# Output products by pairs, cache rows by way of GpSimd and DRAM copies, and a fixed order for the first up units

## The chip, the cores and the metric

The kernel runs on one core of a Trainium2 chip. Its time is the device time of one execution in microseconds (us), the median of several runs. The engines of a core are TensorE (PE), VectorE (DVE), ScalarE (ACT), GpSimd (POOL) and SyncE (SP). SP computes nothing; it issues DMAs, as POOL and ACT also can. Each engine works through its own instructions in a fixed order and waits at the first one whose inputs are not there.

## What is computed

The reference is one layer of a streaming encoder over 1024 prompt frames and 64 sample frames (1088 tokens, width 1024), in float32:

```python
xn = rmsnorm(x, g_mix)
cb, cc, ch, q, k, v, ga, gb = split(xn @ w_in)          # widths 6 x 512, 2 x 1024
ya = (cb * causal_conv(cc * ch, prefix)) @ w_conv_out
o  = band_attention(q, k_all, v_all, rel_bias)          # 8 heads of 64, own chunk and 8 before
yb = o @ w_attn_out
x  = x + (sigmoid(ga) * ya + sigmoid(gb) * yb) @ w_out
h  = rmsnorm(x, g_ffn)
x  = x + (silu(h @ w_ff1) * (h @ w_ff3)) @ w_ff2
y  = rmsnorm(x, g_final)
```

For the sample frames, keys and values are 512 cached rows followed by the 64 new ones. The newest 512 rows of each are outputs too (`cache_k_sample`, `cache_v_sample`): 448 old rows and 64 new ones.

## The kernel before, in words

Every operand is held as two float32r halves, a rounded one and a rest, and every product is three matmuls (rounded by rounded, and the two mixed ones). `split` (L120) makes the halves: a cast on ACT (L122), then a subtraction on DVE (L123).

The big products use a Strassen scheme with seven products in place of eight. `STEPS` (L128) orders them 1, 2, 6, 7, 5, 4, 3; each is 24 matmuls of 272 columns in `run` (L240). `Unit` loads 256 columns of a weight matrix into one of two `raw` buffers (L180), and `Unit.prep` (L192) makes the sums and splits of each step's weights. Banks of PSUM carry the keys A, B and D; a bank that is added to again must first have been copied out (`shot`, L226). The steps 6, 7 and 5 use the sums `xs` or `tt` of the tokens' four quarters.

Phase 1 (L485 to L759) normalises nine token tiles, computes v, and then runs twelve units: q, k, cc, ch, gb and cb. The SBUF block `scr` is cut by hand into places: SNAP, STAGE (four slots for rows on their way to DRAM), CC and UT (two slots each); `slot` (L331) hands a list's places out in turn. In the units of q and k, `cache_load` (L681) brings 128 old cache rows into a UT slot by way of SP. `cache_tile` (L686) stores them to the cache outputs (L691, POOL) and writes split v rows (`put_v`, L344, through a CC slot) and transposed, split k rows (L700, through the next CC slot) to DRAM. Beside units 4 and 5, `bias_tables` (L113) loads a table for two heads (L117) into a STAGE slot and stores it to DRAM (L118), both on SP. Fourteen `warm` matmuls run before the first tile (L504); `pvv` is the product for v (L475), for which `whv` holds weights.

Phase 2 (L762 to L1020) computes gates (`gate`, L771: four pieces of 272 columns, each evacuated by ACT at L779 into one of two `st` buffers and stored by POOL at L780) and interleaves the attention (L949). Before the last three gate blocks it loads the conv branch u (L1005), the attention rows o (L1008) and the softmax factors rc (L1012, two buffers), and makes the operand `ob` of their product (L1015, L1016). `gates_in` (L975) loads the gates back.

Phase 3 (L1025 to L1044) merges: for each of eight blocks m of 128 channels, four pieces ya (12 matmuls each, 48 in all) from the conv branch, then four pieces yb from `ob`. DVE multiplies them with the gates, adds, and the sum is split into `mg` (and `ms` for the sample tokens). `plan` (L313) lists the weights in the order of use; `next_w` prepares one product ahead of the block in use.

Phase 4 multiplies with w_out (L1084), adds the residual, normalises (`second`, L1129; L1143) and transposes the tiles again (`turned`, L1146; `xt`, L1153). `second_half` (L1172) makes the sums of quarters; for the tiles at columns 256 and 384 most of them are put off (`rest`). The memory pool `wp` holds what this needs; afterwards `hp` reuses its memory.

Phase 5 is the up stage: 22 units, alternately of w_ff1 (a0, a1, ...) and w_ff3 (b0, b1, ...), the first two started while the last two token tiles are still on their way (L1399 to L1422). Products of the two (`hidden_done`, L1234) are combined, split into `hq` (three buffers) and stored to `h_d` by POOL (L1245). Phase 6 is the down stage (L1526), whose weights lie in `ring` parts (L1284), four of 1024 columns in each ring; part 3 is first filled for pair 3, in the second half of the first block.

The order of each engine's instructions is not the order of the text. A planner orders them when the kernel is built: each instruction becomes ready, by the planner's own estimates of durations, when its inputs and buffers are there, and each engine takes the ready one that stands first in the text. `tc.issue_after(x)` holds the instructions of its block behind x on x's own engine. Buffers of a pool can be taken when each earlier tile on the same memory has been released.

Of the kernel before, what the change touches and what calls it, by code (L numbers as in the profile page):

```python
# [15 lines left out]
P = 128  # L16
# [22 lines left out]
WARM = 14  # L39
# [26 lines left out]
def encoder_kernel(ctx: ExitStack, tc: tile.TileContext, ins, outs):  # L66
# [46 lines left out]
    def bias_tables(j, t):  # L113

        t = t.rearrange("p (h n) -> p h n", h=2)
        src = ins["bias_ext"][2 * j, 384:]
        nc.sync.dma_start(t, bass.AP(tensor=src.tensor, offset=src.offset, ap=[[0, P], [768, 2], [1, 384]]))  # L117
        nc.sync.dma_start(bias_d[2 * j : 2 * j + 2].rearrange("h (p n) -> p h n", n=384), t)  # L118

    def split(hi, lo, src):  # L120

        a = act.copy(hi, src)  # L122
        vec.tensor_tensor(lo, src, hi.bitcast(F32), op=ALU.subtract)  # L123
        return a.ins
# [13 lines left out]
    def both(t, c, n, src):  # L138
        split(t[:, 0, :, c : c + n], t[:, 1, :, c : c + n], src)
# [36 lines left out]
    class Unit:  # L176
# [9 lines left out]
        def plain(self, p, src):  # L186
            self.w[p] = [
                ws.tile([P, 4, P], F32R, tag=t, name=f"{t}{self.nm}_{p}") for t in ("wh", "wl")
            ]
            split(*self.w[p], src)  # L190
# [28 lines left out]

    def run(unit, x, banks, snaps, done, ahead):  # L220


        nm = unit.nm
        ps, snap = {}, {}

        def shot(key, src):  # L226
            s = snaps(key, f"s{nm}_{key}").rearrange("p (j n) -> p j n", j=2)
            act.copy(s, src)
            snap[key] = s

        for si, p in enumerate(STEPS):
            key = {1: "A", 6: "A", 5: "A", 3: "A", 2: "B", 7: "D", 4: "D"}[p]
            if key not in ps:
                ps[key] = banks("A" if key == "A" else "BD", f"{key}{nm}")
            t = ps[key]
            hi, lo = unit.w[p]
            for k in range(4):
                for n, (w, l) in enumerate(((hi, 0), (hi, 1), (lo, 0))):
                    for j in range(2):
                        mm(  # L240
                            t[:, j, :HN], w[:, k, :], x[p][:, l, k, j * HN : (j + 1) * HN],
                            start=p in (1, 2, 7) and k == 0 and n == 0,
                            stop=k == 3 and n == 2, skip_group_check=p in (6, 5, 4, 3),
                        )
# [83 lines left out]
    SNAP, STAGE, CC, UT = [544 * i for i in range(5)], [2720, 3808, 9312, 10400], [4896, 5988], [7080, 8172]  # L328
    turn = {}
# [74 lines left out]


# [94 lines left out]
    warm = bank1("A", "warm")  # L500
    ones = mspool.tile([P, 2, 512], F32R, tag="ms", name="ones")[:, 0]
    act.copy(ones, cols[:, 13:14].to_broadcast([P, 512]))
    for n in range(WARM):
        mm(warm[:, n % 2], ones[:, :P], ones, start=True, stop=True)  # L504
# [3 lines left out]
    split_wv(0, mixed[0])  # L508
    split_wv(1, mixed[0])
# [171 lines left out]
    def cache_load(i):  # L681
        cts[i] = ct = slot(UT, 2 * ATT)
        nc.sync.dma_start(ct[:, :ATT], ck[i * P : (i + 1) * P])
        nc.sync.dma_start(ct[:, ATT:], cvv[i * P : (i + 1) * P])

    def cache_tile(i):  # L686
        ct = cts[i]
        a = 0 if i else TS
        row = i * P + a - TS
        for nm, o in (("k", 0), ("v", ATT)):  # L690
            nc.gpsimd.dma_start(outs[f"cache_{nm}_sample"][row : row + P - a], ct[a:, o : o + ATT])  # L691
# [72 lines left out]
    st_pool = pg_stack.enter_context(tc.tile_pool(name="st_pool", bufs=2, reuse_waits="tile"))  # L764
# [210 lines left out]
    def gates_in(m):  # L975
        sg = {}
        for o, n in PIECES:
            for nm, src in (("ga", ga_d), ("gb", gb_d)):
                t = sg[nm, o] = mp.tile([P, HN], F32, tag=nm, name=f"{nm}{m}_{o}")
                nc.sync.dma_start(t, src[m * P : (m + 1) * P, o : o + n])  # L980
        return sg
# [11 lines left out]
    for i in range(4, len(GATES)):  # L993
        gate_w[i] = next_w()
        if i == len(GATES) - LAST:
# [7 lines left out]
            sg = gates_in(0)  # L1003
            for k in range(4):
                nc.sync.dma_start(u.t[:, :, k].bitcast(F32), u_d[k])  # L1005
            for k in range(4):
                o = ob.t[:, 0, k].bitcast(F32)
                nc.sync.dma_start(o, o_d[k * P : (k + 1) * P])  # L1008
                r = mp.tile([P, T], F32, tag="rc", name=f"rc{k}", bufs=2)
                for j in range(2):  # L1010
                    src = rc_d[2 * k + j]
                    nc.sync.dma_start(  # L1012
# [12 lines left out]
    for m in range(8):  # L1025
        wa, wb = next_w(), next_w()
        if m:
            sg = gates_in(m)
        for o, n in PIECES:
            for nm in ("ga", "gb"):  # L1030
                act.activation(sg[nm, o], sg[nm, o], AF.Sigmoid)
            ya = psum2.tile([P, 512], F32, tag="mm", name=f"ya{m}_{o}")
            product(ya[:, :n], wa, u, o, n)
            vec.tensor_tensor(sg["ga", o], ya[:, :n], sg["ga", o], op=ALU.mult)
        for o, n in PIECES:
            t = sg["ga", o]
            yb = psum2.tile([P, 512], F32, tag="mm", name=f"yb{m}_{o}")
            product(yb[:, :n], wb, ob, o, n)
            vec.tensor_tensor(sg["gb", o], yb[:, :n], sg["gb", o], op=ALU.mult)
            vec.tensor_tensor(t, t, sg["gb", o], op=ALU.add)  # L1040
            split(mg.at(0, m, o, n), mg.at(1, m, o, n), t)
            h, a = o // HT, 512 - o % HT
            if a < n:
                split(ms[:, m, 0, 32 * h : 32 * h + 32], ms[:, m, 1, 32 * h : 32 * h + 32], t[:, a:])  # L1044
# [66 lines left out]
    if True:  # L1111
# [17 lines left out]
        def second(i):  # L1129
# [13 lines left out]
            vec.scalar_tensor_tensor(xg[:n], xt[:n], r[:n], gb_row[:n], op0=ALU.mult, op1=ALU.mult)  # L1143
# [26 lines left out]
        rest = []  # L1170

        def second_half(src, c, n):  # L1172
# [8 lines left out]
            def others():  # L1181
                minus(f[:, 0], s[:, 1], f[:, 0])
                both(tt[7], c, n, f[:, 0])
                both(tt[5], c, n, s[:, 0])
                minus(f[:, 1], f[:, 1], s[:, 1])
# [4 lines left out]
            both(tt[6], c, n, s[:, 1])  # L1190
            both(ax[1, 1], c, n, src[:, 1])
            if c in (256, 384):
                rest.append(others)
            else:
                others()
# [19 lines left out]

    names = [(l, p) for p in range(NF // 2) for l in "ab"]
    sa = {}

    def gate_done(p):
        def f(r, h, src, snap):  # L1220
# [9 lines left out]
            act.activation(out, out, AF.Silu)  # L1230
# [3 lines left out]
    def hidden_done(p):  # L1234
# [4 lines left out]
        def keep(c, x):  # L1239
            if hp is None:  # L1240
                waiting.append(lambda: keep(c, x))
                return
            hq = hp.tile([P, 4, 2, P], F32R, tag="hq", name=f"hq{p}_{c}", bufs=3)
# [6 lines left out]
        def f(r, h, src, snap):  # L1250
# [4 lines left out]
            else:  # L1255
                vec.tensor_tensor(snap, src, snap, op=ALU.add)
                vec.tensor_tensor(two, snap, two, op=ALU.mult)  # L1257
# [145 lines left out]
    next(r0)  # L1403
    next(r0)
# [18 lines left out]
    for n in range(1, len(names)):  # L1423
# [3 lines left out]
        else:  # L1427
# [3 lines left out]
            refill()  # L1431
        if n == 1:
# [176 lines left out]
```

## Time and profile before

| what | value |
| --- | --- |
| median of three runs | 1498.62 us (1498.4 to 1502.81) |
| the profiled execution | 1501.25 us |
| its span, first to last instruction | 1499.5 us |
| granted TensorE clock, mean | 0.999 |
| HBM read, written | 171.06 MB, 91.92 MB |
| DMA issues from POOL and others in software | 62.71 MB |
| DMA issues from SP and others in hardware | 198.23 MB |

A view of waits has, for each waiting instruction, its engine, the tile it writes and its line, whom it waited for, and the total, number and longest of its waits in us. A timeline row has its start, its length, the engine, line, operation, tiles written and read, shapes and count; the bracket holds the idle time of the engine before it and what ended it. Rows whose engine ends in q are of a sequencer, as all of SP are. A matmul's length includes its way through the array; the next one starts earlier.

### The profile page before, as it was taken

To read this page: it belongs to the slowest core of one execution; us is meant where nothing else is said; L and a number is where in the kernel's file an instruction comes from. 1 tells how busy PE (TensorE), PEld (TensorE's weight loads), DVE (VectorE), ACT (ScalarE), POOL (GpSimd) and SP (SyncE) were. 2 spreads that over 40 slices of the span, in tenths; PEclk is the share of its full clock that TensorE was granted. 3 is DMA by queue.
4 is the path that set the end of the run, shared out by engine and by line. 5 is a ranking of instruction groups with operands and counts; after the bars stand their busy time and mean duration, and the time that the engine had idled before them with its cause. 6 is when DMAs were issued, how large, how long until landed. Compare 5 with 4: busy or idle time off the path is not lost.

```text
span 1499.5 us, 26494 instructions
## 1 busy us (share of the span) xinstructions
PE 1472.1 (98%) x10192; PEld 1380.2 (92%) x10192; DVE 980.9 (65%) x1852; ACT 682.1 (45%) x1398; POOL 128.8 (9%) x236
## 2 busy tenths in 40 slices
PE   8999999999999999999999999999999999999997
PEld 6899999999999998998889999999999999788886
DVE  7975466633776743863489676666666668757577
ACT  7654333334776662541356444444444445403123
POOL 1300010001111111000000111100011011000000
PEclk9999999999999999999999999999999999999999
DMA  8696613178776538655432444433344438767675
GB/s 288 188 313 215 194 54 122 58 216 220 189 191 179 144 94 278 185 150 170 151 113 78 144 142 148 149 139 117 118 154 147 156 141 309 250 231 233 229 262 204
DMA packets 167518, 264.73 MB, mean 177 GB/s; under 512 B 19008, under 2 KB 103168, under 8 KB 167264
## 3 DMA queue, kind: packets, MB, share of 16 engines
q1 hardware_dynamic: 146736, 198.23, 42.7%
q0 software_dynamic: 19504, 62.71, 11.5%
q10 hardware_dynamic: 1152, 2.10, 0.4%
q8 instruction: 80, 1.31, 0.4%
q14 instruction: 46, 0.38, 0.1%
HBM read 171.06 MB, written 91.92 MB: 175 GB/s over the span
## 4 chain that ended last, share of the span: by engine, by line
issue 44%; PE 43%; POOL 4%; DMA 4%; DVE 3%; ACT 1%; SPq 1%; POOLq 0%; ACTq 0%; DVEq 0%
PE A L1526 7%; PE D L1526 3%; POOL h_d L1245 3%; PE B L1526 2%; PE t L918 2%; PE Acb L240 2%; PE Ach L240 2%; PE Ak L240 2%; PE g L302 2%; PE g L303 2%; PE Agb L240 2%; PE g L304 2%; PE pv L943 1%; PE Aq L240 1%; PE s L871 1%
## 5 line engine op out<-in xcount | busy, mean ns | idle before, releaser
L1526 PE MATMUL A<-ring,ht 128*128 128x512 f32 x528 | 124.6, 390 | 1.7 <-ACT acc L1536 1.1
L1526 PEld LDWEIGHTS A<-ring,ht 128*128 128x128 f32 x528 | 98.8, 188 | 23.3 <-ACT acc L1536 1.5
L302 PE MATMUL g<-xn,whp 128*128 128x272 f32 x384 | 113.0, 294 | 0.9 <-ACT gst L779 0.9
L303 PE MATMUL g<-xn,whp 128*128 128x272 f32 x384 | 111.8, 291 | 0.0
L304 PE MATMUL g<-xn,wlp 128*128 128x272 f32 x384 | 111.1, 289 | 0.0
L122 ACT CAST ring<-w2r 128x512 fp32r<-128x512 f32 (+1 forms) x78 | 43.4, 587 | 99.9 <-PE A L1526 50.7
L122 ACT CAST hq<-sa 128x512 fp32r<-128x512 f32 x77 | 47.7, 620 | 88.0 <-DVE sa L1257 54.1
L1245 POOL DMA_DIRECT2D h_d<-hq x77 | 41.0, 532 | 417.2 <-DVE hq L123 216.3
L123 DVE TENSOR_TENSOR hq<-sa,hq 128x512 fp32r<-128x512 f32 x77 | 53.2, 691 | 36.0 <-ACT hq L122 35.8
L829 DVE CUSTOM_DVE_ANT_0 p<-s,bb 128x640 f32<-128x640 f32 (+5 forms) x72 | 47.5, 661 | 43.2 <-DMA qd<-q_d 28.1
L302 PEld LDWEIGHTS g<-xn,whp 128*128 128x128 f32 x384 | 72.3, 188 | 2.1 <-ACT gst L779 1.1
L304 PEld LDWEIGHTS g<-xn,wlp 128*128 128x128 f32 x384 | 72.3, 188 | 0.5
L303 PEld LDWEIGHTS g<-xn,whp 128*128 128x128 f32 x384 | 72.4, 189 | 0.3
L123 DVE TENSOR_TENSOR wla<-rawa,wha 128x512 fp32r<-128x512 f32 x56 | 38.5, 688 | 40.5 <-ACT wha L122 40.5
L240 PE MATMUL Aa<-tt,wha 128*128 128x272 f32 x352 | 59.1, 289 | 3.7 <-ACT tt L122 2.5
L1526 PE MATMUL D<-ring,ht 128*128 128x512 f32 x264 | 62.6, 389 | 0.0
L1526 PEld LDWEIGHTS D<-ring,ht 128*128 128x128 f32 x264 | 49.6, 188 | 10.3
L240 PE MATMUL Ab<-mg,whb 128*128 128x272 f32 x352 | 58.4, 288 | 0.0
L240 PE MATMUL Aa<-mg,wha 128*128 128x272 f32 x352 | 58.3, 288 | 0.0
L240 PE MATMUL Ab<-tt,whb 128*128 128x272 f32 x352 | 58.3, 288 | 0.0
L122 ACT CAST wha<-rawa 128x512 fp32r<-128x512 f32 x56 | 34.8, 621 | 51.3 <-PE Ab L240 35.5
L123 DVE TENSOR_TENSOR ring<-w2r,ring 128x512 fp32r<-128x512 f32 (+1 forms) x78 | 48.7, 649 | 12.0 <-ACT ring L122 12.0
(522 smaller groups left out, 4369.8 us busy)
## 6 DMA issues: line engine op xcount, KB each, us to landing
h_d<-hq POOLq DMA_DIRECT2D x77, 512.0 KB, 3.7
ht<-h_d SPq DMA_DIRECT2D x154, 256.0 KB, 3.7
w2r<-in_w_ff SPq DMA_DIRECT2D x11, 1024.0 KB, 5.6
rawa<-in_w_ff SPq DMA_DIRECT2D x11, 1024.0 KB, 5.8
rawb<-in_w_ff SPq DMA_DIRECT2D x11, 1024.0 KB, 5.4
qd<-q_d SPq DMA_DIRECT2D x32, 272.0 KB, 4.8
rawp<-in_w_in SPq DMA_DIRECT2D x6, 1024.0 KB, 6.6
u_d<-scr SPq DMA_DIRECT2D x8, 544.0 KB, 5.3
```

The costliest lines, as they stand in the source:

```text
L122: a = act.copy(hi, src)
L123: vec.tensor_tensor(lo, src, hi.bitcast(F32), op=ALU.subtract)
L240: mm(t[:, j, :HN], w[:, k, :], x[p][:, l, k, j * HN : (j + 1) * HN], start=p in (1, 2, 7) and k == 0 and n == 0, stop=k == 3 and n == 2, s ...
L302: mm(out, a, p, start=k == 0, stop=False)
L303: mm(out, a, q, start=False, stop=False)
L304: mm(out, b, p, start=False, stop=k == kt - 1)
L829: vec.tensor_tensor_reduce(out=s if len(ps.shape) == 2 else s.rearrange("p (a b) -> p a b", a=2), in0=ps, in1=bias if len(ps.shape) == 2 e ...
L871: mm(ps[:r, i, :w], q[0][:, q0 : q0 + r], k[:, ksl], start=True, stop=False)
L918: nc.tensor.transpose(tp[:, i * P : (i + 1) * P], s[:, i * P : (i + 1) * P], ident)
L943: mm(pv[:, :, lo:hi], v[:, kb, :], pt[:, :, kb - base, lo:hi], start=i == 0, stop=i == len(blocks) - 1,)
L1245: nc.gpsimd.dma_start(h_d[p, c - 1], hq.rearrange("p i l t -> p (i l t)").bitcast(F32))
L1526: mm(t, ht[k][:, j, x], w[:, l], start=p in (1, 2, 7) and k == 0 and n == 0, stop=k == len(ks) - 1 and n == 2, skip_group_check=p in (6, 5 ...
```

## The change

It makes these edits:

- **Start.** The 14 warm matmuls stand earlier in the text. Eight transposes of the identity into `warm` follow the transposes of the first tile.
- **Bias tables.** Load and store are separate; the stores come one unit later (units 5 and 6).
- **Places in `scr`.** STAGE has three slots in place of four; CC has three in place of two, and its turn starts at the third.
- **Caches.** Cache rows are loaded by POOL in place of SP. The eight stores of old rows from SBUF go; two copies from DRAM to DRAM stand in the up stage in front of unit 4.
- **Gates.** Five `st` buffers in place of two.
- **Output products.** Blocks m are taken in pairs: ya of both, then yb of both; the weights are listed to match. Gate tiles have eight (ga) and four (gb) buffers. Before the phase only ga of block 0 is loaded ahead of u, o and rc; ga of block 1 and gb of block 0 come behind the last rc load. rc has three buffers in place of two.
- **First up units.** The two late tiles are turned after the first and the second step of a0. Step 6's weights of a0 stay behind the last normalisation; the deferred sums stay behind the last tile's `tt` for step 6 and come in three forms, each followed by a step's weights; the first Silu and product stay behind a later cast; the rest of a0 stays behind the last matmul of b0's second step.
- **Last up unit.** Four of its seven `hq` tiles lie in part 3 of the rings of 1, 2, 6 and 7.

```diff
-WARM = 14
+WARM = (14, 8)
...
+    for n in range(WARM[1]):
+        nc.tensor.transpose(warm[:, 0, :P], ident, ident)
     split_wv(0, mixed[0][0])
...
-        plan += [(ld, 4, j * P) for j in range(2) for ld in lds]
+        plan += [(ld, 4, j * P) for ld in lds for j in range(2)]
...
-    SNAP, STAGE, CC, UT = [544 * i for i in range(5)], [2720, 3808, 9312, 10400], [4896, 5988], [7080, 8172]
-    turn = {}
+    SNAP, STAGE, CC, UT = [544 * i for i in range(5)], [2720, 3808, 9312], [4896, 5988, 10400], [7080, 8172]
+    turn = {tuple(CC): 1}
...
-        nc.sync.dma_start(ct[:, :ATT], ck[i * P : (i + 1) * P])
-        nc.sync.dma_start(ct[:, ATT:], cvv[i * P : (i + 1) * P])
+        nc.gpsimd.dma_start(ct[:, :ATT], ck[i * P : (i + 1) * P])
+        nc.gpsimd.dma_start(ct[:, ATT:], cvv[i * P : (i + 1) * P])
...
-        for nm, o in (("k", 0), ("v", ATT)):
-            nc.gpsimd.dma_start(outs[f"cache_{nm}_sample"][row : row + P - a], ct[a:, o : o + ATT])
...
+        if n in (5, 6):
+            for j in range(2):
+                table_store(2 * (n - 5) + j)
         if n in (4, 5):
             for j in range(2):
-                bias_tables(2 * (n - 4) + j, slot(STAGE, 768))
+                table_load(2 * (n - 4) + j, slot(STAGE, 768))
...
-    st_pool = pg_stack.enter_context(tc.tile_pool(name="st_pool", bufs=2, reuse_waits="tile"))
+    st_pool = pg_stack.enter_context(tc.tile_pool(name="st_pool", bufs=5, reuse_waits="tile"))
...
-            sg = gates_in(0)
+            gates_in("ga", 0)
...
+            with tc.issue_after(ld.ins):
+                gates_in("ga", 1)
+                gates_in("gb", 0)
...
-    for m in range(8):
-        wa, wb = next_w(), next_w()
...
+    for m0 in range(0, 8, 2):
+        for m in (m0, m0 + 1):
+            wa = next_w()
...
+        for m in (m0, m0 + 1):
+            wb = next_w()
...
+            if p == NF // 2 - 1 and c in LATE:
+                hq = ring_of(LATE[c])[:, 3072:4096].rearrange("p (i l t) -> p i l t", i=4, l=2)
+            else:
+                hq = hp.tile([P, 4, 2, P], F32R, tag="hq", name=f"hq{p}_{c}", bufs=3)
...
     next(r0)
+    turned(*late.pop(0), "BD")
     next(r0)
     turned(*late.pop(0), "BD")
...
-    turned(*late.pop(0), "BD")
     next(r1)
-    for f in rest:
-        f()
-    wp_stack.close()
-    hp = ctx.enter_context(tc.tile_pool(name="hp", bufs=2, reuse_waits="tile"))
-    for f in waiting:
-        f()
-    for st in range(2, len(STEPS)):
-        u0.prep(st)
-    for _ in r0:
-        pass
+    with tc.issue_after(normed2[-1]):
+        u0.prep(2)
+    with tc.issue_after(urgent[0]), tc.issue_after(urgent[1]):
+        for forms, st in zip(zip(*rest), (3, 4, 5)):
+            for form in forms:
+                form()
+            u0.prep(st)
+            if st == 3:
+                silu = u0.cast
+        wp_stack.close()
+        hp = ctx.enter_context(tc.tile_pool(name="hp", bufs=2, reuse_waits="tile"))
+        u0.prep(6)
+        with tc.issue_after(silu):
+            for f in waiting:
+                f()
+    with tc.issue_after(newest[0]):
+        for _ in r0:
+            pass
...
+        if n == 4:
+            for nm, src in (("k", ck), ("v", cvv)):
+                nc.gpsimd.dma_start(outs[f"cache_{nm}_sample"][: CACHE - TS], src[TS:])
```

More of the change, by code (lines that the diff above doesn't have):

```diff
@@ L138, in both @@
     def both(t, c, n, src):
-        split(t[:, 0, :, c : c + n], t[:, 1, :, c : c + n], src)
+        return split(t[:, 0, :, c : c + n], t[:, 1, :, c : c + n], src)
     def column(i):
@@ L403, in normed @@
             vec.scalar_tensor_tensor(xt[:n, c], xt[:n, c], r[:n], gm[:n, c], op0=ALU.mult, op1=ALU.mult)
+    warm = bank1("A", "warm")
+    ones = mspool.tile([P, 2, 512], F32R, tag="ms", name="ones")[:, 0]
+    act.copy(ones, cols[:, 13:14].to_broadcast([P, 512]))
+    for n in range(WARM[0]):
+        mm(warm[:, n % 2], ones[:, :P], ones, start=True, stop=True)
     xs8 = mspool.tile([P, KD, TS * 2], F32R, tag="ms", name="xs8")
@@ L498, in unit_of @@
         return Unit(src, f"{nm}{u}")
[L500 to L504, printed above, removed]
     normed(ORDER[0])
@@ L973, in between, with gates_in @@
             next(steps, None)
-    def gates_in(m):
-        sg = {}
+    sg = {}
+    def gates_in(nm, m):
         for o, n in PIECES:
[L978 to L981, printed above, removed]
+            t = sg[nm, m, o] = mp.tile([P, HN], F32, tag=nm, name=f"{nm}{m}_{o}", bufs=8 if nm == "ga" else 4)
+            nc.sync.dma_start(t, (ga_d if nm == "ga" else gb_d)[m * P : (m + 1) * P, o : o + n])
     head_load(0)
@@ L1189, in second_half @@
             minus(s[:, 1], src[:, 1], s[:, 0])
-            both(tt[6], c, n, s[:, 1])
-            both(ax[1, 1], c, n, src[:, 1])
+            if c == 256:
+                both(ax[1, 1], c, n, src[:, 1])
+            urgent[:] = both(tt[6], c, n, s[:, 1])
+            if c != 256:
+                both(ax[1, 1], c, n, src[:, 1])
             if c in (256, 384):
-                rest.append(others)
+                rest.append((seventh, fifth, fourth))
             else:
-                others()
+                for form in (seventh, fifth, fourth):
+                    form()
         late = []
@@ L1229, in f @@
             vec.tensor_tensor(out, src, snap, op=ALU.add)
-            act.activation(out, out, AF.Silu)
+            if hp is None:
+                waiting.append(lambda: act.activation(out, out, AF.Silu))
+            else:
+                act.activation(out, out, AF.Silu)
         return f
@@ L1256, in f @@
                 vec.tensor_tensor(snap, src, snap, op=ALU.add)
+                if hp is None:
+                    waiting.append(lambda: vec.tensor_tensor(two, snap, two, op=ALU.mult))
+                    waiting.append(lambda: keep(1, x))
+                    return
                 vec.tensor_tensor(two, snap, two, op=ALU.mult)
```

85 lines of the change are left out of this document (46 added, 39 removed).

## The prediction

> **What bounds the kernel now.** I read the page first, then the waits of TensorE, then the timelines around the longest of these waits. The page's busy times (engine, us, share of the span, instructions):
>
> ```profile
> PE 1472.1 (98%) x10192; PEld 1380.2 (92%) x10192; DVE 980.9 (65%) x1852; ACT 682.1 (45%) x1398; POOL 128.8 (9%) x236
> ```
>
> TensorE (PE) is busy for 98%, and the change leaves its matmuls as they are (it adds eight transposes). So the change can win only what PE idles. The waits of PE, longest total first (who, for whom: us, times, longest):
>
> ```profile
> PE warm L504 <- ACT ones L502: 2.9, 1, 2.9
> PE Aa L240 <- ACT tt L122: 2.5, 2, 1.4
> PE Acc L240 <- DVE scr L543: 2.3, 1, 2.3
> PE yb L302 <- ACT ob L122: 1.9, 2, 1.4
> PE Aq L240 <- DVE scr L551: 1.3, 1, 1.3
> PE pvv L475 <- ACT whv L122: 1.2, 1, 1.2
> PE Aa L240 <- ACT sa_Q L228: 1.2, 2, 0.6
> PE A L1526 <- ACT acc L1536: 1.1, 1, 1.1
> PE s L871 <- DVE mx L829: 1.0, 3, 0.5
> PE g L302 <- ACT gst L779: 0.9, 1, 0.9
> PE wo L1088 <- DVE ms L123: 0.8, 1, 0.8
> PE A L1526 <- DVE acc L1538: 0.6, 1, 0.6
> PE yb L303 <- DVE ob L123: 0.6, 1, 0.6
> ```
>
> These come to 18.3 us. Not touched are the first (2.9, before the first matmul) and the Aa waits for sa_Q in later units (1.2); the wait of pvv (1.2) is filled, not shortened. What is left, 13.0, is about the ceiling of the change. I go through it in order of time.
>
> **The change part by part.** *Start.* The warm matmuls are traced earlier and eight transposes of the identity are added behind those of the first tile.
>
> ```profile
> 2.94 5.79 PE L504 MATMUL warm<-ones 128*128 128x512 f32 x14 [2.94 <-ACT ones L502]
> 10.86 1.04 PE L417 MATMUL xt<-ident,scr 128*128 128x128 f32 x8
> ```
>
> The warm matmuls wait for the ScalarE (ACT) copy of `ones`, not for their place in the text, so that move is worth 0. Eight transposes take at most 1.04 us and fall into the 1.2 us in which PE waits for whv: cover for all of them. If they came behind that wait instead, they would cost 0.9 (eight pitches of about 0.11). Bounds -0.3 to +0.9; I take 0.
>
> *Cache rows.* A cache row block passes through two CC slots, and a slot must have been stored before it is filled again.
>
> ```profile
> 108.60 0.62 ACT L122 CAST scr<-scr 128x512 fp32r<-128x512 f32 x1 [4.74 <-DMA v_d<-scr]
> ```
>
> ACT stood 4.74 us for such a store; VectorE (DVE) stood behind ACT, and PE behind DVE for the 1.3 of Aq. With three slots the fourth block's v goes where the second block's k lay, no longer where the third block's v is still being stored. Loads move from SP's queue to GpSimd's (POOL), which loses the eight copies to the output; an issue there costs little:
>
> ```profile
> L691 POOL DMA_DIRECT2D out_cache_v_sample<-scr x4: 535/556/579, 48.2 to 94.5; - x4
> ```
>
> Behind a waiting cache load POOL has only the conv state's transfers, which belong to later units. Bounds 0 to -1.3; I take -1.3. (The Trainium skill, DMA: Bandwidth & Descriptors, section SWDGE vs HWDGE vs iDMA, says that GpSimd writes its descriptors into SBUF and that VectorE can lock it out. The row above varies by 0.04 us beside a busy DVE, so the trace does not bear a penalty out.)
>
> *Bias tables.* SP issued each table's store right behind its load and waited for the landing; the weights of gb stood behind that. From the waits of SP, and the timelines of SP and DVE:
>
> ```profile
> SPq L118 <- DMA scr<-in_bias_ext: 7.2, 4, 3.0
> ```
> ```profile
> 165.27 1.41 SPq L117 DMA_DIRECT2D scr<-in_bias_ext  x2
> 166.73 0.46 SPq L180 DMA_DIRECT2D rawgb<-in_w_in  x1
> ```
> ```profile
> 176.79 0.69 DVE L197 TENSOR_TENSOR sf<-rawgb 128x512 f32<-128x512 f32 x1 [4.46 <-DMA rawgb<-in_w_in]
> ```
>
> rawgb took 10.1 us from issue to use; DVE idled 4.46, and PE 2.3 (Acc). Stores one unit later take up to 3.0 us of SP's wait away ahead of rawgb, more than the 2.3. But STAGE shrinks from four slots to three, so the fourth table's load must now wait until the first table's store has landed, with rawgb behind it on SP. Bounds 0 to -2.3; I take -1.3.
>
> *Gates and output products.*
>
> ```profile
> 580.50 0.39 ACT L779 COPY gst<-g 128x272 f32<-128x272 f32 x1 [7.37 <-DMA gb_d<-gst]
> ```
> ```profile
> 584.38 1.08 SPq L1012 DMA_DIRECT2D rc<-rc_d  x2
> 585.51 0.59 SPq L1008 DMA_DIRECT2D ob<-o_d  x1
> 590.04 1.08 SPq L1012 DMA_DIRECT2D rc<-rc_d  x2
> ```
>
> Two st slots made ACT wait 7.37 us for a gate piece's store; five cover 15 us of PE (a piece is 24 matmuls of 0.125, the pitch of the PE rows further below: 3.0 us). The 0.9 goes. The ob operands came late because rc's third and fourth loads waited for two rc slots. Now there are three; half of the first gate loads move behind rc; and PE does a second ya product (48 matmuls, 6.0 us) before the first yb needs ob. 6.0 covers the 1.9 + 0.6, and the split of the first attn_out weights, which moves one product later. What could be late next is the ga load of m=1, issued behind the last rc load; five PSUM slots hold its products meanwhile. The last wait, wo for ms (0.8), follows DVE's queue at the tail; ga loads come earlier by pairs: -0.4. Together -3.8, bounds -0.9 to -4.2. Freeing ACT of gst waits also helps the attention steps (s, 1.0): -0.5, bounds 0 to -1.0.
>
> *First units of the up stage.* Busy times from 785 to 815 (PE, PEld, DVE, ACT, POOL), and four timeline rows:
>
> ```profile
> 785.00:815.00 30.00, 27.50 (x209) 26.40 (x208) 29.64 (x54) 19.99 (x38) 1.08 (x2) 1.00 0.19 63
> ```
> ```profile
> 793.90 0.69 DVE L197 TENSOR_TENSOR sf<-rawb 128x512 f32<-128x512 f32 x1
> 794.50 1.28 DVE L1143 SCALAR_TENSOR_TENSOR xg<-x,some,gb_row 128x1024 f32<-128x1024 f32 x1
> ```
> ```profile
> 809.15 0.69 DVE L123 TENSOR_TENSOR mg<-kept,mg 128x512 fp32r<-128x512 f32 x1
> ```
>
> DVE is full here; PE's 2.5 (Aa for tt) is DVE's debt. A 512-wide DVE operation has a pitch of 0.60 (793.90 to 794.50). The last tile's normalisation (794.50) stood behind five weight splits of unit a0 that are now held behind it: it comes 5 x 0.60 = 3.0 us sooner. PE also gets b0's second step (24 matmuls, 3.0) ahead of the step that waited, and ACT loads the Silu table only behind the first deferred forms. So the 2.5 goes. But it can be given back one step later. Step 5 of a0 (p = 5 in L128's order) needs the copy sa_Q, which lies in hp, and hp reuses the memory of the deferred forms:
>
> ```profile
> 810.32 0.62 ACT L122 CAST hq<-sa 128x512 fp32r<-128x512 f32 x1
> 810.84 0.60 ACT L228 COPY sa_Q<-Aa 128x544 f32<-128x544 f32 x1
> ```
> ```profile
> 810.24 0.66 PE L240 MATMUL Ab<-tt,whb 128*128 128x272 f32 x4
> ```
> ```profile
> 811.61 0.67 PE L240 MATMUL Aa<-tt,wha 128*128 128x272 f32 x4
> ```
>
> Both first writes of hp follow the last form's end (809.15 + 0.69). PE filled 810.24 to 811.61 with b0's matmuls; without a filler, step 5 could have begun at 810.24. In the new order about seven DVE operations that stood ahead of the last form stand behind it (two splits and a difference of a0, three sums of b0, one product), and three sums done before 785 come in: four pitches or 2.4 us at most sooner; with DVE waits in the new chain I take half, 1.0. Bounds: -2.5 if hp's memory is free at once, +0.5 if step 5 waits without a filler. I take -1.0.
>
> *Last unit's rows.*
>
> ```profile
> 1264.63 0.62 ACT L122 CAST hq<-sa 128x512 fp32r<-128x512 f32 x1 [2.56 <-DMA h_d<-hq]
> 1266.81 0.62 ACT L122 CAST hq<-sa 128x512 fp32r<-128x512 f32 x1 [1.57 <-DMA h_d<-hq]
> ```
>
> ACT waits 4.1 us for hq slots; four rows now go to ring parts that no one uses yet. PE's 1.1 + 0.6 (A for acc) stood behind these. DVE's work there stays: -1.2, bounds 0 to -1.7. If a row's store is late, the ring's next weights wait; I cost that at 0, since these parts fill only in the first block.
>
> *Copies DRAM to DRAM.* Two of 0.92 MB each (448 rows of 512 floats), on POOL, in the text after the fifth up unit. They need no SBUF, so nothing ties them to that place. The planner does move such work far forward: this load stands behind the up stage in the text.
>
> ```profile
> 677.88 0.39 SPq L1322 DMA_DIRECT2D w2r<-in_w_ff  x1
> ```
>
> In mid-kernel they cost 0; h_d stores queue behind them on POOL. At the start they meet full DMA engines (share, GB/s last):
>
> ```profile
> 8.00:12.00 4.00, 2.70 (x21) 1.84 (x19) 3.28 (x9) 3.14 (x9) 0.00 (x0) 1.00 1.04 393
> ```
>
> 1.84 MB at 393 GB/s is 4.7 us: bounds 0 to +4.7, taken 0.
>
> **The sum.** 1.3 + 1.3 + 3.8 + 0.5 + 1.0 + 1.2 = 9.1 us less. The profiled execution took 1501.25 (span 1499.5), 2.6 above the median of 1498.62; I take the difference off the median: 1489.5.
>
> **The rivals.** *Copies at the start (the change does not do what it says).* For: no dependence, POOL idle there, the w2r row. Against: nothing as loose as these stands in the trace. If they share the engines with the x and wv loads, half of 4.7 is lost, 2.4: 1491.9; all of it: 1494.2. (The Trainium skill, DMA: Bandwidth & Descriptors, section Queues, rings and completion order, says that each DMA engine takes turns between the queues that have work. By it the loads lose a full copy's time, 4.7, and the time is 1494.2; no run here shows the two queues contending at the start.)
>
> *The up stage gives nothing back.* If hp's memory is free in time, 1.5 more: 1488.0. For: ACT had other work at 809 to 810. Against: two first writes of hp, both right behind the last form.
>
> *DVE sets the pace.* Waits whose cause is DVE's queue return elsewhere, and only the merge's transfers win, 3.8: 1494.8. For: 29.64 of 30 us. Against: in the units of the caches and in the merge the first cause is a transfer.
>
> *STAGE of three slots (slower).* q, k and cb write 24 staged rows; a slot comes back after three writes, at the closest four steps of 3.0 us, 12 us. A store of this kind:
>
> ```profile
> q_d<-scr SPq DMA_DIRECT2D x4, 512.0 KB, 7.3
> ```
>
> Landing leaves 4.7 us for SP's queue. If SP is later than that, ACT stands at each write and PE behind it. From 0.4 us a write the 9.1 are gone; at 1 us each the time is 1513.5. Against: SP loses the cache loads that blocked it.
>
> **How the numbers follow.** The forecast 0.40, copies at the start 0.22, nothing given back 0.15, DVE's pace 0.17, STAGE 0.06. The range goes from all favourable bounds (1.3 + 2.3 + 4.2 + 1.0 + 2.5 + 1.7 + 0.3 = 13.3: 1485.3) to 2.2 above the third rival, for copies at the start on top of it (half): 1485.3 to 1497.0. What is left out is STAGE, and the two rivals at their dearest together. A measurement of this kernel tells about 0.3% (4.5 us) from no change. Below 1494.1 lie the forecast, the second rival, most of the first and a little of the third: 0.78. Same: 0.15. Slower: 0.07.
>
> **What would show it.** The wait rows yb for ob and g for gst gone: the merge term. Aq and Acc gone: slots and tables. Aa for tt gone and a new wait of Aa for sa_Q near 807: the give-back. hq without DMA waits near 1264: the rings. The first issue of the copies in POOL's timeline settles the first rival. Wrong altogether would be an ACT wait at L570 or L122 for q_d or k_d stores.

## The result, and the profile after

The changed kernel takes 1508.09 us in the median (1506.26 to 1510.44), the kernel before 1498.51 on the same chip: a ratio of 1.0049, 95% interval 1.0033 to 1.0065. It is slower; the forecast was 9 us less. The profiled execution took 1509.1 us, its span is 1507.3 (before 1501.25 and 1499.5). The page's busy times say as little as before:

```profile
PE 1475.1 (98%) x10200; PEld 1383.1 (92%) x10200; DVE 981.9 (65%) x1852; ACT 682.8 (45%) x1398; POOL 130.0 (9%) x238
```

The waits of PE tell more (who, for whom: us, times, longest):

```profile
PE pvv L487 <- ACT whv L126: 6.7, 1, 6.7
PE xt L429 <- issue: 5.4, 2, 3.7
PE warm L416 <- ACT ones L414: 2.9, 1, 2.9
PE Aa L246 <- ACT sa_Q L234: 2.0, 3, 0.8
PE Dq L246 <- ACT scr L234: 1.6, 1, 1.6
PE A L1571 <- DVE acc L1583: 1.6, 1, 1.6
PE A L1571 <- ACT acc L1581: 1.1, 1, 1.1
PE g L308 <- ACT scr L550: 1.0, 1, 1.0
```

Against the list of before: the waits for tt (2.5), ob (1.9 and 0.6), gst (0.9), ms (0.8) and Acc (2.3) are gone, as forecast. New are 6.7 and 5.4 (3.7 at 12.88 and 1.7 at 45.61), all before the first unit's products. So the loss lies ahead of the first unit, and the rest won. The start, in POOL's timeline:

```profile
1.32 0.63 POOL L1476 DMA_DIRECT2D out_cache_k_sample<-in_cache_k  x1 [0.37 <-issue]
...
2.28 0.55 POOL L1476 DMA_DIRECT2D out_cache_v_sample<-in_cache_v  x1
```

Both copies, which the text has in front of the fifth up unit, are issued some 2 us into the kernel: the first rival has come true, "the change does not do what it says". But its price was to be 2.4 to 4.7. PE, ACT and DVE of the same kernel:

```profile
12.88 1.30 PE L429 MATMUL xt<-ident,scr 64*128 64x64 f32 x8 [3.67 <-issue]
14.12 1.97 PE L516 MATMUL warm<-ident 128*128 128x128 f32 x8
22.75 0.69 PE L487 MATMUL pvv<-whv,xs 128*64 128x512 f32 x1 [6.67 <-ACT whv L126]
```
```profile
13.28 1.06 ACT L394 ACTIVATE scr<-scr 128x1024 f32<-128x1024 f32 x1 [7.01 <-DMA scr<-in_x_prompt]
...
20.00 1.06 ACT L394 ACTIVATE scr<-scr 128x1024 f32<-128x1024 f32 x1 [5.14 <-DMA scr<-in_x_prompt]
...
21.59 0.59 ACT L126 CAST xs<-xt 128x512 fp32r<-128x512 f32 x1
```
```profile
12.04 1.41 DVE L409 SCALAR_TENSOR_TENSOR scr<-scr 64x512 f32<-64x512 f32 x2 [5.15 <-DMA scr<-in_g_mix]
```

Two things are to be seen. First, g_mix lands at 12.04 (its DMA took 10.5 us, 4.3 before), so the first transposes start at 12.88, 4.2 us late. Second, they are done by 14.2, and ACT could have cast xs at 14.85. It does so at 21.59, because in its order the Square of the *third* token tile stands ahead of that cast, and this tile lands only at 20.00. In the kernel before that Square stood behind the casts of whv (it ran at 15.69). The first product for v starts at 22.75 in place of 10.56. The same work of ACT in the kernel before:

```profile
9.41 0.58 ACT L122 CAST xs<-xt 128x512 fp32r<-128x512 f32 x1 [0.48 <-PE xt L417]
...
14.49 1.18 ACT L122 CAST whv<-wv 128x512 fp32r<-128x512 f32 x2
...
15.69 1.10 ACT L388 ACTIVATE scr<-scr 128x1024 f32<-128x1024 f32 x1
```

All kernels here have the same 7632 matmuls of 272 columns, so the start of the n-th says how late a kernel is. The first (tile Aq) starts at 68.48 before and at 83.44 after. The table gives the length of the stages between such marks, in us:

| stage | before | after | difference |
| --- | --- | --- | --- |
| start, to the first unit | 68.48 | 83.44 | +15.0 |
| units of q and k (672 matmuls) | 89.69 | 90.07 | +0.4 |
| units cc0 and ch0 (to 1008) | 45.44 | 42.83 | -2.6 |
| the other six units (to 2016) | 125.88 | 127.01 | +1.1 |
| gates and attention (to 3168) | 254.55 | 252.56 | -2.0 |
| output products to the norms (to 3936) | 203.07 | 198.51 | -4.6 |
| first two up units (to 4272) | 47.18 | 46.22 | -1.0 |
| other up units (to 7632) | 422.51 | 422.53 | 0.0 |
| down stage, to the last matmul | 234.33 | 235.56 | +1.2 |

What follows the last matmul is 0.2 longer; the sum is the span's 7.8.

### The profile page after: what moved, and what is told of

The parts are those of the page before. It is cut to its first block, busy times and chain, and to the rows that moved or that the text cites. A ratio compares the mean times of both kernels' runs of the same rounds, so it can differ in the third digit from the quotient of the medians.

```text
span 1507.3 us, 26483 instructions
## 1 busy us (share of the span) xinstructions
PE 1475.1 (98%) x10200; PEld 1383.1 (92%) x10200; DVE 981.9 (65%) x1852; ACT 682.8 (45%) x1398; POOL 130.0 (9%) x238
## 4 chain that ended last, share of the span: by engine, by line
PE 79%; issue 9%; DVE 5%; DMA 3%; ACT 2%; POOL 1%; SPq 0%; POOLq 0%; ACTq 0%; DVEq 0%
PE A L1571 7%; PE Aa L246 6%; PE Ab L246 6%; PE D L1571 3%; PE Da L246 3%; PE g L308 3%; PE g L309 3%; PE g L310 3%; PE Db L246 3%; PE wo L1101 2%; PE wo L1100 2%; PE wo L1102 2%; PE B L1571 2%; PE t L926 2%; PE Ak L246 2%
```

## The experiments

**Theory T**: the copies at the start cost some 12 us, about 5 as transfers that delay the first loads, about 7 because ACT's built order changes with them. **Rivals**: the other edits at the start cost it (R); the transfers alone do, and the order only shows the wait elsewhere (R2). Times of the kernel before differ between chips by up to 2.7 us, so ratios are compared, each to the kernel before on its own chip. "First unit" is the start of the first 272-column matmul.

| kernel | median us (before) | ratio, 95% interval | first product for v | first unit |
| --- | --- | --- | --- | --- |
| before | | 1 | 10.56 | 68.48 |
| changed | 1508.09 (1498.51) | 1.0049, 1.0033 to 1.0065 | 22.75 | 83.44 |
| copies late | 1493.22 (1500.81) | 0.9955, 0.9943 to 0.9968 | 10.80 | 68.59 |
| copies alone | 1514.88 (1500.81) | 1.0096, 1.0083 to 1.0109 | 22.23 | 83.23 |
| third Square behind | 1502.15 (1500.81) | 1.0008, 0.9998 to 1.0017 | 15.46 | 74.45 |
| copies behind x_d | 1507.18 (1500.81) | 1.0044, 1.0032 to 1.0056 | 10.40 | 81.58 |
| copy of k at the start | 1502.18 (1501.16) | 1.0016, 1.0004 to 1.0028 | 19.68 | 78.51 |
| late, no rows in rings | 1491.36 (1501.16) | 0.9936, 0.9921 to 0.9952 | 10.60 | 68.55 |
| late, first up units as before | 1495.21 (1501.16) | 0.9962, 0.9949 to 0.9975 | 10.30 | 68.29 |
| late, products by single blocks | 1495.36 (1501.16) | 0.9963, 0.9948 to 0.9977 | 10.46 | 68.36 |
| late, places as before | 1494.72 (1500.05) | 0.9963, 0.9950 to 0.9976 | 11.08 | 68.72 |
| late, tables as before | 1492.28 (1500.05) | 0.9941, 0.9929 to 0.9954 | 10.87 | 68.70 |
| late, cache rows by SP | 1491.63 (1500.05) | 0.9941, 0.9929 to 0.9953 | 11.08 | 68.73 |
| late, no rows, no fillers | 1490.88 (1500.05) | 0.9935, 0.9923 to 0.9947 | 10.37 | 68.34 |

### Copies late

```diff
-            nc.gpsimd.dma_start(h_d[p, c - 1], ...)
+            stored[0] = nc.gpsimd.dma_start(h_d[p, c - 1], ...).ins
...
-            for nm, src in (("k", ck), ("v", cvv)):
-                nc.gpsimd.dma_start(...)
+            with tc.issue_after(stored[0]):
+                for nm, src in (("k", ck), ("v", cvv)):
+                    nc.gpsimd.dma_start(...)
```

> The changed kernel with one edit: both DRAM copies are held behind the last h_d store of unit b1 on GpSimd. Theory T (the copies at the start cost about 12 us, some 5 by taking the DMA engines from the first x, g_mix and wv loads and some 7 because ScalarE's order then puts the Square of the third token tile ahead of the cast of xs): 1508.1 - 12 = 1496, with first transposes back near 8.7 us and first product for v near 10.6. Rival R (the start loses through its other edits, fillers and earlier warm matmuls, and the copies cost at most their transfer, 4.7): not below 1503.4, first product for v later than 15 us.

The ratio falls from 1.0049 to 0.9955, the span from 1507.3 to 1491.0; the first product starts at 10.80. R has fallen: with fillers and early warm matmuls in place the start is that of before. The copies cost 16.3 us of span, 14.9 of it before the first unit, more than T's 12. They are now issued at 878.00 and 878.51, in the up stage, and cost nothing there that the stages show.

### Copies alone, in the kernel before

```diff
-        for nm, o in (("k", 0), ("v", ATT)):
-            nc.gpsimd.dma_start(outs[f"cache_{nm}_sample"][row : row + P - a], ct[a:, o : o + ATT])
...
+        if n == 4:
+            for nm, src in (("k", ck), ("v", cvv)):
+                nc.gpsimd.dma_start(outs[f"cache_{nm}_sample"][: CACHE - TS], src[TS:])
```

> The kernel before with one part of the change alone: the eight stores of old cache rows from SBUF go, and the two DRAM copies stand in the up stage, tied to nothing. T: they are issued at the start here too, 1498.5 + 12 = 1510.5, first product for v near 22.7 us. R: at most the transfer, 1498.5 + 4.7 = 1503.2, first product for v at 15.3 at the latest.

1.0096, the first unit at 83.23: this one edit makes the whole loss of the start (14.8 of 15.0), in a kernel that has nothing else of the change.

### The third Square behind the casts

```diff
-                    split(hi, lo, wv_raw[half][:, k])
+                    last_cast[0] = split(hi, lo, wv_raw[half][:, k])[0]
...
-        if n + 2 < len(ORDER):
+        if n == 0:
+            with tc.issue_after(last_cast[0]):
+                normed(ORDER[n + 2])
+        elif n + 2 < len(ORDER):
             normed(ORDER[n + 2])
```

> The changed kernel, copies at the start as they are, with one edit: the normalisation of the third token tile (its Square on ScalarE) is held behind the last cast of the weights for v, where it stood in the kernel before. T: only the transfers' part is left, 1508.1 - 7 = 1501, first product for v near 15.5 us. R2 (the transfers alone cost the 12, the order only shows the wait in another place): 1508, first product for v still near 22 us, waiting for wv or g_mix.

With the copies where they were, ACT now goes on at once:

```profile
12.71 1.06 ACT L394 ACTIVATE scr<-scr 128x1024 f32<-128x1024 f32 x1 [6.86 <-DMA scr<-in_x_prompt]
13.67 0.18 ACT L394 ACTIVATION_READ_ACCUMULATOR scr<-scr 128x1 f32 x1
14.08 0.20 ACT L398 ACTIVATE scr<-scr 128x1 f32<-128x1 f32 x1 [0.22 <-DVE scr L397]
14.31 0.59 ACT L126 CAST xs<-xt 128x512 fp32r<-128x512 f32 x1
```

The first product starts at 15.46 and the first unit at 74.45, 9.0 us sooner than in the changed kernel. R2 has fallen: 9.0 of the 15.0 come of the order (T: 7). The other 6.0 are put down to the transfers: 4.9 up to the first product, where the prediction's bound, 1.84 MB at 393 GB/s, was 4.7. The Trainium skill (DMA: Bandwidth & Descriptors, section Queues, rings and completion order) has each DMA engine take turns between its queues; that the loads lose the copies' whole time agrees with it. The last 1.1, between the first product and the first unit, fits TensorE's lower clock (last section); no run isolates it.

### One copy at the start

The cut is against "copies late":

```diff
-            with tc.issue_after(stored[0]):
-                for nm, src in (("k", ck), ("v", cvv)):
-                    nc.gpsimd.dma_start(...)
+            nc.gpsimd.dma_start(outs["cache_k_sample"][: CACHE - TS], ck[TS:])
+            with tc.issue_after(stored[0]):
+                nc.gpsimd.dma_start(outs["cache_v_sample"][: CACHE - TS], cvv[TS:])
```

> The copies held late, with one edit: the copy of k (0.92 MB) is tied to nothing again, that of v stays late. In the built order it is issued at the start, and ScalarE's order again puts the Square of the third token tile ahead of the cast of xs. T (order 9, transfers 6 for both copies, at the first unit's start): the order's part stays, less the 2 to 3 us by which the third tile lands earlier, the transfers' part halves: first unit 9 to 10 us later than with both late, time 9 us over it. R2 (the cost goes with the bytes): half of 15, 7.5; R4 (one queue's turn, any copy costs the same): 15.

```profile
16.92 1.06 ACT L394 ACTIVATE scr<-scr 128x1024 f32<-128x1024 f32 x1 [5.22 <-DMA scr<-in_x_prompt]
...
18.52 0.58 ACT L126 CAST xs<-xt 128x512 fp32r<-128x512 f32 x1
```

The first unit is 9.9 us later than with both late, the ratio 0.6% higher (about 9 us): T's number; R2's 7.5 and R4's 15 are not met. Half the bytes cost two thirds of the time, since the order is turned by one copy as by two, and the tile that ACT waits for lands at 16.92 in place of 20.00.

### Copies behind the first x_d store

```diff
-            for nm, src in (("k", ck), ("v", cvv)):
+            with tc.issue_after(first_x[512]):
+                for nm, src in (("k", ck), ("v", cvv)):
```

> The changed kernel with the two copies held behind the first x_d store on GpSimd (about 15 us in the kernel before), so that they meet the later x loads and the first weights in place of the first loads. T: the first tiles are free of them; 1496 plus what the later x loads lose, 0 to 3, so 1496 to 1499. R3 (any 1.84 MB in the first 40 us costs its transfer time, since the DMA engines are full there): 1496 + 4.7 = 1500.7.

Both expectations were too low: 1.0044, hardly better than at the start. The copy of k goes out at 16.59, that of v only at 49.98. Nothing is late before the first product (10.40), but PE stands later on, behind DVE:

```profile
41.39 1.12 PE L429 MATMUL xt<-ident,scr 128*128 128x128 f32 x8 [2.66 <-DVE scr L409]
45.64 0.79 PE L487 MATMUL pvv<-whv,xn 128*128 128x512 f32 x1 [3.13 <-DVE scr L127]
```
```profile
42.98 1.41 DVE L409 SCALAR_TENSOR_TENSOR scr<-scr 128x512 f32<-128x512 f32 x2
44.31 0.68 DVE L127 TENSOR_TENSOR xn<-xt,xn 128x512 fp32r<-128x512 f32 x1
44.91 0.68 DVE L127 TENSOR_TENSOR scr<-pvv,scr 128x512 fp32r<-128x512 f32 x1
```

The splits of finished products for v stand behind the normalisation of two later tiles (L409); with the copies late, DVE did such a split at 38.80, ahead of both. So the built order has turned here too, with one copy of 0.92 MB issued by then. How much of the 13.1 us is order and how much transfer this run does not separate.

### The last unit's rows

```diff
-    LATE = {7: 1, 5: 2, 6: 6, 3: 7}
+    LATE = {}
```

> The copies held late, with one edit: the last unit's rows all go through hq as in the kernel before, none into the rings. With both late, TensorE loses 3.7 us at the start of the down stage (waits for acc 1.6, 1.1 and 1.0) against 1.7 in the kernel before. Theory U (the freed rows are stored in one bunch, beside the w2r load that the third step of pair 3 needs, and that load lands later): the 2.1 go, 2 us faster than with both late. Rival V (the waits come of ScalarE and VectorE, not of the rows): no change, and the acc waits stay at 3.7.

The waits of ACT for hq that the prediction quoted are gone with the rings, but another comes: rows of ACT with the copies late, and without the rings.

```profile
1263.42 1.14 ACT L126 CAST ring<-w2r 128x512 fp32r<-128x512 f32 x2 [5.01 <-DMA w2r<-in_w_ff]
```
```profile
1260.03 1.14 ACT L126 CAST ring<-w2r 128x512 fp32r<-128x512 f32 x2 [0.58 <-DMA w2r<-in_w_ff]
```

With the rings the last four h_d stores leave within 4 us (POOL at 1250.26 to 1253.97), without them two of them wait until 1253.93 and 1256.19. The w2r load that ACT needs next is issued at 1253.13 with the rings, behind three of the four stores; without them at 1251.11, ahead of the last two. The DMA engines are full in both (share 1.0). In all ten kernels with the rings ACT waits 3.5 to 5.0 for this load, in the four without at most 0.6. Against the kernel before the down stage grew by 2.3 with the rings and 0.4 without. Over all traces: 235.2 to 236.6 in the ten kernels with the rings, 234.3 to 235.3 in the four without. PE's waits for acc fall from 3.7 to 2.3 without the rings (1.7 before); the other kernels with the rings have 2.6 to 3.5. So the late load is shown, and U's direction with it, at about 1 us in the mean rather than 2. That it costs time is less sure: two of the four kernels without the rings lack most of the change, and the ratios, 0.9936 against 0.9955, have overlapping intervals.

### The first up units as before

The edit puts the text of the kernel before back for the deferred sums, `hidden_done` and the order of the first two up units.

> The copies held late, with one part undone: the first two units of the up stage ordered as in the kernel before. If the fixed order wins what the forecast said: the waits of Aa for tt (2.5) are back and the one for sa_Q near 800 us (0.8) goes: 1 to 2 us slower than with both late. Rival (VectorE sets the pace there, the win came of the earlier arrival): no change.

```profile
PE Aa L246 <- ACT tt L126: 2.5, 2, 1.4
```

The 2.5 is back, and the first two up units take 47.18 us, to the hundredth what they take before; with the fixed order 46.23. So the order wins 0.95, and the rival has fallen.

### Output products by single blocks

The edit puts back the plan, `gates_in`, two rc slots and the loop over single blocks; the five `st` buffers stay.

> The copies held late, with one part undone: output products by single blocks, gates and weights loaded as in the kernel before, two rc buffers; the five st buffers stay. Forecast's term without the 0.9 of gst: the yb waits (2.5) and wo (0.8) are back in place of the 1.4 that is left: 2 to 3 us slower than with both late. Rival (the five st buffers alone bring the ob operands early enough): under 1 us.

```profile
PE yb L308 <- ACT ob L126: 1.0, 1, 1.0
PE yb L309 <- DVE ob L127: 0.6, 1, 0.6
```

The stage takes 202.42 us, against 198.48 to 198.59 in six of the seven kernels with copies late and pairs, and 203.07 before. So this part of the change wins 3.9 there, more than the 2 to 3 expected; the waits listed make 1.6 of it. The one exception is the profiled execution of "copies late" itself, 200.48 with 1.4 of yb waits, so its span is some 2 us worse than this form's others. Against that one execution the difference is 1.9, and the ratios, 0.9963 and 0.9955, do not tell the two kernels apart. The rival's share is 0.65.

### Places, tables, cache rows

```diff
-    SNAP, STAGE, CC, UT = ..., [2720, 3808, 9312], [4896, 5988, 10400], ...
-    turn = {tuple(CC): 1}
+    SNAP, STAGE, CC, UT = ..., [2720, 3808, 9312, 10400], [4896, 5988], ...
+    turn = {}
```

> The copies held late, with one part undone: four STAGE and two CC slots as in the kernel before. Forecast's term (the third CC slot takes the wait of Aq away): the wait of 1.3 us near 115 us is back, first gate block 1.3 later than with both late. Rival STAGE (three slots make ScalarE wait for stores in the units of q, k and cb): four slots win, first gate block earlier than with both late.

```diff
-        if n in (5, 6):
-            for j in range(2):
-                table_store(2 * (n - 5) + j)
...
                 table_load(2 * (n - 4) + j, slot(STAGE, 768))
+                table_store(2 * (n - 4) + j)
```

> The copies held late, with one part undone: each table is stored right behind its load on SP, as in the kernel before. Forecast's term: the Acc wait is back, 1.3 to 2.3 us near 180 us. Rival (the three STAGE slots or SP's freedom from the cache loads took it away): no wait of Acc, first gate block at the same time.

```diff
-        nc.gpsimd.dma_start(ct[:, :ATT], ck[i * P : (i + 1) * P])
-        nc.gpsimd.dma_start(ct[:, ATT:], cvv[i * P : (i + 1) * P])
+        nc.sync.dma_start(ct[:, :ATT], ck[i * P : (i + 1) * P])
+        nc.sync.dma_start(ct[:, ATT:], cvv[i * P : (i + 1) * P])
```

> The copies held late, with one part undone: cache rows are loaded by SP, not GpSimd. Forecast's term put the 1.3 on the slots, not on the queue: no change up to the first gate block. Rival (SP's queue was what held the weights): 1 to 2.5 us later by the first gate block.

Two of the three came out against the forecast's causes. With the tables as before, Acc does not wait; with the *places* as before it waits again:

```profile
PE Acc L246 <- DVE scr L552: 1.6, 1, 1.6
```

DVE shows why, first with the places as before, then with the copies late:

```profile
174.74 0.69 DVE L201 TENSOR_TENSOR sf<-rawgb 128x512 f32<-128x512 f32 x1 [3.71 <-DMA rawgb<-in_w_in]
...
176.69 0.72 DVE L552 TENSOR_TENSOR scr<-Acc,scr 128x544 f32<-128x544 f32 x1
```
```profile
174.52 0.72 DVE L552 TENSOR_TENSOR scr<-Acc,scr 128x544 f32<-128x544 f32 x1
...
176.96 0.69 DVE L201 TENSOR_TENSOR sf<-rawgb 128x512 f32<-128x512 f32 x1 [1.12 <-DMA rawgb<-in_w_in]
```

rawgb comes no sooner. But the copy of Acc, which PE waits for, now stands ahead of the sum that waits for rawgb. Once more it is an order that moved, here to the good: with the places as before the units cc0 and ch0 take 44.68 us, 1.85 longer than with the copies late, of the 2.6 won. The run undoes STAGE and CC together, so it does not say which of the two lists turned the order.

The Aq wait did not come back with two CC slots (units of q and k: 88.15), so the third slot is not what removed it; in "third Square behind", which has three slots, PE waits 2.1 for it. In "copies alone", with two slots and SP's loads, the wait is 0.3: of the change that kernel has only the copies in place of the eight stores. Its start is disturbed, so it hints at these stores and does not show them as the cause. With the cache rows by SP these units took 90.00, ACT waiting 4.23 for a cache row, and the first gate block comes 2.0 later, as the rival has it. But 90.11 is also found with products by single blocks, where the rows go by GpSimd and ACT waits 4.88 for a k_d store. The remaining kernels with the start undisturbed have 88.1 to 88.4. One profile each does not settle what GpSimd's loads are worth; the time by SP (0.9941) is no worse than that with GpSimd (0.9955).

### Without the fillers

```diff
-WARM = (14, 8)
+WARM = (14, 0)
```

> The copies held late and no rows in the rings, with one more edit: the eight transposes of the identity at the start go. Forecast's term 0 (bounds -0.3 to 0.9): the first product for v and the first unit start within 0.3 us of the same kernel with them; rival (they hold TensorE's clock through its wait for whv): first unit 0.3 to 1 us later without them.

0.9935 against 0.9936, the first unit at 68.34 against 68.55: no difference, as forecast.

## Why the prediction was wrong

**Copies DRAM to DRAM: the step that failed.** It said 0, from their place in the text (in front of the fifth up unit; the prediction says after it), with an upper bound of 4.7 in case the planner issued them at the start. They are issued at the start, and cost 15.0 us up to the first unit. The bound was near for what it counted, the transfers: 4.9 to the first product. It did not count that every engine's order is planned with the copies in it. ACT's order then put the Square of a tile that lands late ahead of a cast that was ready: 9.0. That the copies changed the order is shown by one edit (copies alone) and that the order costs 9.0 by another (third Square behind); that it is the planner's estimate of later loads that turned it is only the likely reason. The row of w2r had shown that the planner moves loose work far forward; the move got a chance of 0.22 all the same.

**The rest of the sum, 9.1, came out near as a sum, in part by luck.** With the copies late the time is 0.45% less (0.32% to 0.57%, 4.8 to 8.5 us); the span is 8.4 less, in an execution that lost 2 in the output products. But 1.7 of the 8.4 lie in the other up units, which no term covers and which vary from 420.8 to 422.9 us between kernels with the same text there (before 422.5), and terms that were too small make up for one of the wrong sign:

- Start 0: right (no fillers: no change).
- Cache rows -1.3: with the start undisturbed the stage is 1.3 to 1.6 shorter in six of eight kernels, but not by the third CC slot. The size was right there, the cause was not, and it stays open.
- Bias tables -1.3: -2.6, not by the later stores (with them undone no wait comes back); 1.85 of it go with the new places, by DVE's order. The reason given against, a fourth load that waits, costs nothing that is seen.
- Gates and output products -3.8, attention -0.5: -4.6 for the output products and -2.0 for gates and attention (PE's wait for gst lay there), so 6.6 for 4.3. The waits named are gone and the pairs bring 3.9. That the five st buffers bring the 2.0 is not shown: no run undoes them alone, and "copies alone", with two, takes 253.03 us there, 1.5 less than before.
- First up units -1.0: -0.95. The give-back is there: 0.8 of Aa for sa_Q, and 0.5 of Da for its weights, against 2.5 gone.
- Last unit's rows -1.2: about +1 (the time of the whole kernel does not settle it). ACT's waits for hq went, but these had spread the stores out; their bunch delays the w2r load. The step costed a late store at 0 and never asked what the stores would collide with.

**The other rivals.** "DVE sets the pace" fell with the first up units (0.95 was won there). "Nothing given back" fell. "STAGE of three slots" fell: with the places as before, four slots among them, the Acc wait was back.

## A version that is faster than both

The copies held behind an h_d store and the last rows in hq give 0.9936 (0.9921 to 0.9952) of the kernel before, 0.6% less; without the fillers it is 0.9935 (0.9923 to 0.9947). With the rings and the copies late, "copies late" has 0.9955 and the two kernels with the tables and the cache rows as before have 0.9941, so a gain is shown for the late copies, not for hq.

## What to carry to other kernels

Work that depends on nothing is placed by the planner, not by the text: tie it to an instruction beside which it shall run, or count it where it can first go. In a kernel whose queues are fixed when it is built, price a new transfer twice, by its bytes and by what it does to the order of the engines: look in each queue for an instruction that waits for a load and stands ahead of one that is ready. A wait that is taken away may have spread transfers out; ask which load the freed stores will meet.

## What the runs showed of the hardware

TensorE's clock went down when TensorE stood idle for some 3 us. After the change, windows (length, PE busy, PEld, DVE, ACT and POOL busy, granted clock, DMA share, GB/s):

```profile
8.00:12.00 4.00, 1.22 (x4) 0.46 (x2) 0.00 (x0) 0.00 (x0) 0.00 (x0) 1.00 0.62 174
12.00:16.00 4.00, 3.12 (x16) 2.56 (x16) 2.57 (x7) 1.35 (x3) 0.00 (x0) 0.55 1.04 391
16.00:20.00 4.00, 0.08 (x1) 0.00 (x0) 0.95 (x2) 0.00 (x1) 0.00 (x0) 0.50 0.97 375
20.00:24.00 4.00, 1.25 (x5) 1.07 (x6) 2.45 (x7) 2.97 (x6) 0.00 (x0) 0.50 0.02 6
24.00:28.00 4.00, 4.00 (x17) 2.54 (x16) 4.00 (x10) 3.69 (x11) 0.44 (x1) 0.74 0.31 119
```
```profile
25.40 0.63 PE L489 MATMUL pvv<-whv,xs 128*64 128x512 f32 x1
25.83 0.51 PE L487 MATMUL pvv<-whv,xs 128*64 128x512 f32 x1
26.18 0.39 PE L488 MATMUL pvv<-wlv,xs 128*64 128x512 f32 x1
26.40 0.40 PE L489 MATMUL pvv<-whv,xs 128*64 128x512 f32 x1
```

PE's warm matmuls end at 9.22 (8.00 plus the 1.22 that are busy). The granted clock is 1.00 up to 12 us and 0.55 in the mean from 12 to 16. As a step from 1.00 to 0.50 this is a fall near 12.4, some 3.2 us after PE stopped. It is 0.50 from 16 to 24 us, and its 0.74 from 24 to 28 is a rise near 26.1, some 3.3 us after the first product (22.75). The products for v start 0.43 us apart at the lower clock (25.40 to 25.83), then 0.22 (26.18 to 26.40). The eight fillers start at 14.12, when the clock is already down: they take 1.97 us, with the copies late 1.09. So no run here shows whether they would hold a clock that is still up. The Trainium skill (TensorE: Matmul & The Clock Gate, section Part 1: The HAM clock gate) has the clock fall to half after an idle window of some 3.4 us; the trace agrees with the half and nearly with the length.

The waits at the start were thus followed by a smaller loss. In "third Square behind" four gaps between products, from 17.63 to 19.26, are 0.48, 0.43, 0.43 and 0.29 us, then 0.23; from first product to first unit it takes 58.99 us, before 57.92.
